# A hybrid RWKV-7 layer on one core: the recurrent chain's VectorE and ScalarE operations placed 400 places further forward by the scheduler

## The chip, the cores and the metric

The kernel runs on one core of a Trainium2 chip. The metric is the device time of one execution in microseconds, taken as the median of several runs. A profiled execution gives the trace, in which every instruction of the engines has its start and its duration. The engines are called PE (TensorE, the matrix engine), DVE (VectorE), ACT (ScalarE), POOL (GpSimd) and SP (SyncE, which issues most transfers). Each works through its own queue of instructions in the order in which the program writes them.

## What is computed

One layer of a decoder on 1024 tokens of width 1024. The normalised input goes through one large projection, whose columns feed three branches: an RWKV-7 time mixing (16 heads of 64), a convolution module and a cross-attention into 256 memory tokens. The branches are projected, gated, summed and projected once more. What matters here is the time mixing, which is a recurrence over tokens:

```python
def wkv7_scan(r, decay, k, v, a_vec, b_vec):
    def step(state, inp):
        r_t, w_t, k_t, v_t, a_t, b_t = inp
        sa = jnp.einsum('bhvk,bhk->bhv', state, a_t)
        state = (state * w_t[:, :, None, :]
                 + sa[..., :, None] * b_t[:, :, None, :]
                 + v_t[..., :, None] * k_t[:, :, None, :])
        y = jnp.einsum('bhvk,bhk->bhv', state, r_t)
        return state, y
    _, ys = lax.scan(step, s0, seqs)
...
    h = rms_norm(x, g_norm)
    proj = h @ w_all
...
    wkv = wkv7_scan(rh, decay, kh, vh, -kk, kk * ah)
    wkv = (wkv - mu) * lax.rsqrt(var + RWKV_GN_EPS)
    y_rwkv = ((wkv * gn_g + gn_b + bonus) * jax.nn.silu(rwkv_gate)) @ w_proj_rwkv
```

## The kernel before

**Dense work.** The projections are done tile by tile by `g_dense`: a tile of 128 output columns for 1024 tokens in two halves of 512, each half 24 matmuls of 128x128 by 128x512 (L291, result d). Each weight tile is split into a high part wh (ACT, L123) and a low part wl (DVE, L124, 128x1024), and three products of parts are summed. Of the next tile's weights, wl is made while the tile before is multiplied.

**The recurrence.** It is computed in chunks of 64 tokens. The heads go in pairs j = 0 to 7 and the 1024 tokens in halves e = 0 and 1, so there are 16 blocks, numbered 2j + e, with eight chunks each. Four generators write the work of a block:
- `g_prep` makes the decayed r, k and their products: L480 and L486 (decays), L515 to L534 (ar, u, bk, ks, rs) on DVE, L529 and L533 on POOL, L545 on PE.
- `g_sub` solves the triangular systems inside the chunks. POOL scales U by rb (L574, 128x1024). Then DVE does 31 steps of two small operations, tm = W x U (L580) and W += tm (L583). Transposes (L600) and two groups of small matmuls (L608, L618) follow, with copies on ACT.
- `g_pre` prepares the chain's operands for four chunks at a time (L633 to L673).
- `g_chain` carries the 64x64 state s through the chunks: ry = s x ar on PE (L702), sav = ry + Y on DVE (L703), sas = sav x tk on PE (L710), and the new s on DVE (L713, two halves), with sp = s x pc on ACT (L706). After four chunks come the output's matmuls (L724) and their copy (L726). At the block's end the head's mean and variance are made on DVE (L731 to L748), the inverse root on POOL (`rsqrt`, L114 and L118), and DVE normalises Y (L753, L754); PE transposes it (L759), and DVE makes o from it (L761, L762), which is stored.

**What sets the order.** Beside a block's chain run the solve of the next block, the preparation of the one after it and some tiles of dense work. The function `mix` asks the generators in turn for a piece, by their shares of the stage. This is the order in which the instructions are written. A scheduler then takes them from a heap, the lowest number first, among those whose operands come from instructions already placed; the number is the place in which an instruction was written, and inside `tc.high_priority(n)` it is n lower. What comes out is the fixed order of each engine's queue. Behind the recurrence, from some 1080 us of the trace on, come the convolution, the attention and the last projections.

Of the kernel before, what the change touches and what calls it, by code (L numbers as in the profile page):

```python
# [12 lines left out]
AF = mybir.ActivationFunctionType  # L13
ALU = mybir.AluOpType
# [4 lines left out]
P = 128  # L19
# [5 lines left out]
C = 64  # L25
# [33 lines left out]
N_VEC = _n  # L59


@with_exitstack
def hybrid_kernel(ctx: ExitStack, tc: tile.TileContext, x: bass.AP, mem: bass.AP, wt: bass.AP,
                  vecs: bass.AP, wup: bass.AP, gfin: bass.AP, out: bass.AP):
    nc = tc.nc
    act, dve, pool, pe = nc.scalar, nc.vector, nc.gpsimd, nc.tensor


    const = ctx.enter_context(tc.tile_pool(name="const", bufs=1))
# [259 lines left out]
    with tc.tile_pool(name="rk", bufs=1, reuse_waits="tile") as rk:  # L329
# [53 lines left out]
        def fl(ap):  # L383
            return ap.rearrange("p a t -> p (a t)")
# [243 lines left out]
        state = [0]  # L628

        def g_pre(j, e, q, g, bk, v, Y):  # L630
            tkp = bank("tr")
            for cc in range(4):
                pe.transpose(tkp[:, cc * P:(cc + 1) * P], fl(bk[:, q * 4 + cc, :, :]), ident)  # L633
            tk = rk.tile([P, 4, P], F32, name="tk", tag="tk", bufs=2)
            act.copy(tk, tkp.rearrange("p (c t) -> p c t", t=P))
            yield
            vtp = bank("tr")
            for cc in range(2):
                c = q * 4 + cc * 2
                pe.transpose(vtp[:, cc * P:(cc + 1) * P], v[:, c * C:(c + 2) * C], ident)  # L640
            sav = rk.tile([P, 4, P], F32, name="sav", tag="sav", bufs=2)
            for par in range(2):
                rows = slice(ko(par), ko(par) + C)
                act.copy(sav[rows, par::2, :], vtp[rows, 0:2 * P].rearrange("p (c t) -> p c t", t=P))
            yield
            zv = vtp[:, 2 * P:4 * P]
            u1 = bank("g", 2)
            uv = u1.rearrange("p (k c h t) -> p k c h t", k=2, c=2, h=2)
            for n in range(4):
                cc2, hh = n // 2, n % 2  # L650
                vsl = slice(hh * C, (hh + 1) * C)
# [16 lines left out]
            act.copy(fl(Y[:, q * 2:q * 2 + 2, :]), zv)  # L668
            for par in range(2):
                own = slice(so(par), so(par) + C)  # L670
                oth = slice(ko(par), ko(par) + C)
                act.copy(tk[own, par::2, :], uv[own, 0].rearrange("p c h t -> p c (h t)"))
                act.copy(g[own, par, :, q * 2:q * 2 + 2, oth], uv[own, 1].rearrange("p c h t -> p h c t"))  # L673
            yield (tk, sav)

        def g_chain(j, e):
            g, ar, bk, pc = GG.pop((j, e)), AR.pop((j, e)), BK.pop((j, e)), PCS.pop((j, e))
            v = VS.pop((j, e))
            if e == 0:
                dve.memset(s0[state[0]], 0.0)  # L680
# [10 lines left out]
            dve.tensor_tensor(out=bv, in0=bp, in1=v, op=ALU.mult)  # L691
            for q in range(2):
                tk, sav = got
                ry = bank("ry", 2)
                for cc in range(4):
                    c = q * 4 + cc
                    par = c % 2
                    cg = e * CPH + c
                    own = slice(so(par), so(par) + C)
                    cs = slice(cc * P, (cc + 1) * P)  # L700
                    S0, S1 = s0[state[0]], s0[1 - state[0]]
                    pe.matmul(ry[:, cs], lhsT=fl(ar[:, c, :, :]), rhs=S0, start=True, stop=True)  # L702
                    dve.tensor_tensor(out=sav[own, cc, :], in0=ry[own, cs], in1=Y[own, c // 2, :], op=ALU.add)  # L703
                    if cg < NCH - 1:
                        sp = rk.tile([P, P], F32, name="sp", tag="sp", bufs=1)
                        act.activation(sp, S0, AF.Copy, scale=pc[:, c:c + 1])  # L706
                    yield
                    if cg < NCH - 1:
                        sn = bank("sas")
                        pe.matmul(sn[:, 0:P], lhsT=tk[:, cc, :], rhs=sav[:, cc, :], start=True, stop=True)  # L710
                        for hh in range(2):
                            vsl = slice(hh * C, (hh + 1) * C)
                            dve.scalar_tensor_tensor(out=S1[vsl, vsl], in0=sn[vsl, vsl], scalar=pc[vsl, c:c + 1],  # L713
                                                     in1=sp[vsl, vsl], op0=ALU.mult, op1=ALU.add)
# [11 lines left out]
                act.copy(fl(Y[:, q * 2:q * 2 + 2, :]), yp[:, 0:2 * P])  # L726
                yield
                ryv = ry.rearrange("p (c t) -> p c t", t=P)
                for par in range(2):
                    oth = slice(ko(par), ko(par) + C)  # L730
                    dve.tensor_tensor(out=Y[oth, q * 2:q * 2 + 2, :], in0=Y[oth, q * 2:q * 2 + 2, :],  # L731
                                      in1=ryv[oth, par::2, :], op=ALU.add)
                for c2 in range(q * 2, q * 2 + 2):
                    for hh in range(2):
                        dve.bn_stats(out=st[:, c2, hh, :], in_=Y[:, c2, hh * C:(hh + 1) * C])
                yield

            n2 = CPH
# [4 lines left out]
            dve.tensor_tensor(out=mn, in0=stv[:, :, 1], in1=stv[:, :, 4], op=ALU.add)  # L743
            dve.tensor_tensor(out=df, in0=stv[:, :, 1], in1=stv[:, :, 4], op=ALU.subtract)
            dve.tensor_scalar(out=mn, in0=mn, scalar1=0.5, scalar2=None, op0=ALU.mult)
            dve.tensor_tensor(out=vr, in0=stv[:, :, 2], in1=stv[:, :, 5], op=ALU.add)
            dve.tensor_tensor(out=df, in0=df, in1=df, op=ALU.mult)
# [499 lines left out]
```

## Time and profile before

| | us |
|---|---|
| median of 3 runs | 1961.04 |
| lowest and highest run | 1960.19, 1962.81 |
| the profiled execution | 1960.84 |
| its span in the trace | 1959.0 |
| PE busy | 1848.2 (94% of the span) |
| DVE busy | 1411.1 (72%) |
| ACT busy | 693.2 (35%) |
| POOL busy | 226.5 (12%) |

The span runs from the first instruction to the last; 1.84 us of the execution lie outside it. An engine's busy time leaves out the time in which it waits. In the trace a PE matmul's duration reaches over the start of the next one, since they are pipelined; the distance from start to start is what it costs. In the rows of the timelines, a bracket at the end is the time that the engine was idle before the instruction, and what ended the wait.

### The profile page before, as it was taken

Reading aid. Unit: us, or ns where it says so; the run is one execution under the profiler, and the core shown is the slowest. Engines: PE = TensorE matmul, PEld = TensorE weight load, DVE = VectorE, ACT = ScalarE, POOL = GpSimd, SP = SyncE. Lnnn points to the kernel's source line nnn. Section 1 sums busy time; section 2 is a strip of 40 time slices with the busy share of each in tenths; the row PEclk is TensorE's granted clock in tenths of the full one; section 3 lists DMA queues with packets and bytes.
Section 4 is the critical chain, followed back from the end, with each engine's and each line's share of the span. In section 5 each row is a group of like instructions: output and inputs, shape, how many; then the busy total and the mean of one; then the engine's idle time right before and its main releaser. Section 6 shows DMA issues by size and latency. Waiting matters only on the chain. (4 is left out here: it accounts for less than half of the span.)

```text
span 1959.0 us, 30018 instructions
## 1 busy us (share of the span) xinstructions
PE 1848.2 (94%) x11412; PEld 1472.8 (75%) x11412; DVE 1411.1 (72%) x3028; ACT 693.2 (35%) x1303; POOL 226.5 (12%) x311
## 2 busy tenths in 40 slices
PE   6999998989899899989999999999999999999998
PEld 5777766767676676667788888888888787778887
DVE  6667787777778777787636998898999748644423
ACT  6334343443344344334334313232313435432121
POOL 2201111111111111111000000000000213100001
PEclk9999999999999999999999999999999999999999
DMA  4232212122121212212224411212123646775332
GB/s 147 58 97 63 71 36 68 54 61 68 48 86 36 66 56 58 71 42 79 71 78 140 132 46 42 75 54 76 54 76 108 233 163 221 256 252 164 129 129 86
DMA packets 127936, 188.61 MB, mean 96 GB/s; under 512 B 64432, under 2 KB 66608, under 8 KB 127792
## 3 DMA queue, kind: packets, MB, share of 16 engines
q1 hardware_dynamic: 122704, 178.11, 29.0%
q10 hardware_dynamic: 4768, 8.07, 1.1%
q8 instruction: 89, 1.46, 0.3%
q0 software_dynamic: 320, 0.52, 0.1%
q14 instruction: 55, 0.45, 0.1%
HBM read 139.92 MB, written 46.20 MB: 95 GB/s over the span
## 5 line engine op out<-in xcount | busy, mean ns | idle before, releaser
L291 PE MATMUL d<-hH,wh 128*128 128x512 f32 x1552 | 626.0, 403 | 6.8 <-DVE cg L928 4.4
L291 PE MATMUL d<-hH,wl 128*128 128x512 f32 x1552 | 621.8, 401 | 0.0
L291 PE MATMUL d<-hL,wh 128*128 128x512 f32 x1552 | 619.1, 399 | 0.0
L291 PEld LDWEIGHTS d<-hH,wh 128*128 128x128 f32 x1552 | 294.1, 189 | 63.6 <-DVE cg L928 5.7
L291 PEld LDWEIGHTS d<-hH,wl 128*128 128x128 f32 x1552 | 294.1, 190 | 59.4 <-issue 0.2
L291 PEld LDWEIGHTS d<-hL,wh 128*128 128x128 f32 x1552 | 294.1, 189 | 56.2 <-issue 0.2
L841 DVE SCALAR_TENSOR_TENSOR ac<-up,wdw,ac 128x1024 f32<-128x1024 f32 x240 | 308.2, 1284 | 11.8 <-ACT ac L838 6.0
L123 ACT CAST wh<-wf 128x1024 fp32r<-128x1024 f32 x137 | 143.6, 1049 | 324.1 <-PE d L291 304.3
L124 DVE TENSOR_TENSOR wl<-wf,wh 128x1024 fp32r<-128x1024 f32 x137 | 176.8, 1291 | 95.7 <-ACT wh L123 95.4
L291 PE MATMUL d<-oH,wh 128*128 128x512 f32 x384 | 152.5, 397 | 11.4 <-DVE mg L1101 7.4
L291 PE MATMUL d<-oH,wl 128*128 128x512 f32 x384 | 151.4, 394 | 0.0
L291 PE MATMUL d<-oL,wh 128*128 128x512 f32 x384 | 151.4, 394 | 0.0
L583 DVE TENSOR_TENSOR W<-W,tm 128x60 f32<-128x60 f32 (+24 forms) x496 | 112.4, 227 | 10.0
L580 DVE TENSOR_TENSOR tm<-W,U 128x60 f32<-128x60 f32 (+24 forms) x496 | 107.7, 217 | 11.1
L706 ACT ACTIVATE sp<-s,pc 128x128 f32<-128x128 f32 x120 | 48.3, 402 | 174.8 <-DVE s L713 137.6
L291 PEld LDWEIGHTS d<-oH,wh 128*128 128x128 f32 x384 | 72.9, 190 | 30.4 <-ACT y L1138 5.1
L710 PEld LDWEIGHTS sas<-sav,tk 128*128 128x128 f32 x240 | 38.4, 188 | 67.5 <-DVE sav L703 49.2
L710 PE MATMUL sas<-sav,tk 128*128 128x128 f32 x240 | 54.1, 307 | 34.1 <-DVE sav L703 32.4
L291 PEld LDWEIGHTS d<-oH,wl 128*128 128x128 f32 x384 | 72.8, 190 | 16.1
L291 PEld LDWEIGHTS d<-oL,wh 128*128 128x128 f32 x384 | 72.8, 189 | 15.4
L713 DVE SCALAR_TENSOR_TENSOR s<-sas,pc,sp 64x64 f32<-64x64 f32 x240 | 67.6, 282 | 21.5 <-PE sas L710 16.1
L703 DVE TENSOR_TENSOR sav<-ry,Y 64x128 f32<-64x128 f32 x128 | 36.8, 288 | 43.4 <-ACT Y L668 26.5
(277 smaller groups left out, 2608.7 us busy)
## 6 DMA issues: line engine op xcount, KB each, us to landing
wf<-in_wt_dram SPq DMA_DIRECT2D x137, 512.0 KB
g_d<-gt SPq DMA_DIRECT2D x48, 256.0 KB
U<-ud SPq DMA_DIRECT2D x64, 128.0 KB
nxt<-in_x_dram SPq DMA_DIRECT2D x8, 512.0 KB
o_rwkv_d<-o SPq DMA_DIRECT2D x16, 256.0 KB
cv_d<-ac SPq DMA_DIRECT2D x8, 512.0 KB
o_mem_d<-om SPq DMA_DIRECT2D x16, 256.0 KB
xs<-cv_d SPq DMA_DIRECT2D x8, 512.0 KB
```

The lines of the kernel that those rows point to most:

```text
L123: act.copy(hi, src)
L124: (eng or dve).tensor_tensor(out=lo, in0=src, in1=hi.bitcast(F32), op=ALU.subtract)
L291: pe.matmul(po, lhsT=l[:, ks_], rhs=r[:, k, sl], start=(n == 0), stop=(n == 3 * KT - 1))
L580: dve.tensor_tensor(out=tv, in0=W[:, 0:m, i:i + 1].broadcast_to([NG * 32, m, n]), in1=U[:, i:i + 1, i + 1:32].broadcast_to([NG * 32, m, n] ...
L583: dve.tensor_tensor(out=wv_, in0=wv_, in1=tv, op=ALU.add)
L703: dve.tensor_tensor(out=sav[own, cc, :], in0=ry[own, cs], in1=Y[own, c // 2, :], op=ALU.add)
L706: act.activation(sp, S0, AF.Copy, scale=pc[:, c:c + 1])
L710: pe.matmul(sn[:, 0:P], lhsT=tk[:, cc, :], rhs=sav[:, cc, :], start=True, stop=True)
L713: dve.scalar_tensor_tensor(out=S1[vsl, vsl], in0=sn[vsl, vsl], scalar=pc[vsl, c:c + 1], in1=sp[vsl, vsl], op0=ALU.mult, op1=ALU.add)
L841: dve.scalar_tensor_tensor(out=ac, in0=up[:, tap:tap + S], scalar=wdw[:, tap * 8 + j:tap * 8 + j + 1], in1=ac, op0=ALU.mult, op1=ALU.add)
```

## The change

The operations of `g_pre` and `g_chain` on DVE and ACT, and the `rsqrt` of `g_chain` on POOL, are each issued inside `tc.high_priority(400)`. The matmuls and the transfers aren't. Since a helper issues them, the wrapped operations have the helper's line L73 in the changed kernel, and the other lines are some 16 higher (L291 is L307, L580 is L596, L702 is L718, L710 is L726, L724 is L740, L759 is L776).

```diff
+AHEAD = 400
...
+class Urgent:
+    def __init__(self, tc, eng):
+        self._tc, self._eng = tc, eng
+
+    def __getattr__(self, op):
+        f = getattr(self._eng, op)
+
+        def call(*args, **kw):
+            with self._tc.high_priority(AHEAD):
+                return f(*args, **kw)
+        return call
...
+    act_u, dve_u, pool_u = Urgent(tc, act), Urgent(tc, dve), Urgent(tc, pool)
...
-            act.copy(tk, tkp.rearrange("p (c t) -> p c t", t=P))
+            act_u.copy(tk, tkp.rearrange("p (c t) -> p c t", t=P))
...
-                    dve.tensor_tensor(out=sav[own, cc, :], in0=ry[own, cs], in1=Y[own, c // 2, :], op=ALU.add)
+                    dve_u.tensor_tensor(out=sav[own, cc, :], in0=ry[own, cs], in1=Y[own, c // 2, :], op=ALU.add)
...
-                        act.activation(sp, S0, AF.Copy, scale=pc[:, c:c + 1])
+                        act_u.activation(sp, S0, AF.Copy, scale=pc[:, c:c + 1])
...
-            dve.scalar_tensor_tensor(out=vr, in0=df, scalar=16.0, in1=vr, op0=ALU.mult, op1=ALU.add)
-            rsqrt(vr, vr, 1.0 / C, GN_EPS)
+            dve_u.scalar_tensor_tensor(out=vr, in0=df, scalar=16.0, in1=vr, op0=ALU.mult, op1=ALU.add)
+            with tc.high_priority(AHEAD):
+                rsqrt(vr, vr, 1.0 / C, GN_EPS)
```

All other operations of the two generators on DVE and ACT are changed in the same way. No instruction is added or removed. Of PE's 9356 instructions 1344 stand at another place of its queue, of DVE's 3030 it is 1207, of ACT's 1273 it is 167, of SP's 781 it is 93 and of POOL's 316 it is 6, all of them inside the recurrence.

The first place is DVE's queue behind the end of block 6, an even one: o is the block's output, tm and W are steps of the solve for a later block, sav and s_0 belong to the chain of the next block. Before:

```order
L762 SCALAR_TENSOR_TENSOR o<-o,vec,sg 128x512
L703 TENSOR_TENSOR sav<-ry,Y 64x128
L580 TENSOR_TENSOR tm<-W,U 128x31
L583 TENSOR_TENSOR W<-W,tm 128x31
L713 SCALAR_TENSOR_TENSOR s_0_405<-sas,pc,sp 64x64
L580 TENSOR_TENSOR tm<-W,U 128x30
```

And now:

```order
L73 SCALAR_TENSOR_TENSOR o<-o,vec,sg 128x512
L596 TENSOR_TENSOR tm<-W,U 128x31
L599 TENSOR_TENSOR W<-W,tm 128x31
L596 TENSOR_TENSOR tm<-W,U 128x30
L599 TENSOR_TENSOR W<-W,tm 128x30
L596 TENSOR_TENSOR tm<-W,U 128x29
L599 TENSOR_TENSOR W<-W,tm 128x29
L596 TENSOR_TENSOR tm<-W,U 128x28
L599 TENSOR_TENSOR W<-W,tm 128x28
L596 TENSOR_TENSOR tm<-W,U 128x54
L73 TENSOR_TENSOR sav<-ry,Y 64x128
```

Nine steps of the solve, which were spread behind the first sav, stand ahead of it.

The second place is PE's queue at the end of block 8: L724 is the output's matmuls, L759 the transposes of the block's end, L702 the first matmul of the next block's chain, and d the dense work. The first rows are those around L724, the last those around L759. Before:

```order
L618 MATMUL tr<-zt,wb 32x32 x16
L291 MATMUL d<-hH,wh 128x512
L291 MATMUL d<-hL,wh 128x512
L291 MATMUL d<-hH,wl 128x512
L291 MATMUL d<-hH,wh 128x512
L724 MATMUL tr<-sav,g 64x64 x8
...
L291 MATMUL d<-hL,wh 128x512
L759 MATMUL tr<-ident,Y 128x128 x4
L702 MATMUL ry<-s_0_405,ar 128x128
```

Between L724 and L759 stand 25 rows of L291. And now, with the middle of it where L718 stands:

```order
L740 MATMUL tr<-sav,g 64x64 x8
...
L307 MATMUL d<-hL,wh 128x512
L718 MATMUL ry<-s_0_405,ar 128x128
L307 MATMUL d<-hH,wl 128x512
L307 MATMUL d<-hH,wh 128x512
L307 MATMUL d<-hL,wh 128x512
L307 MATMUL d<-hH,wl 128x512
L307 MATMUL d<-hH,wh 128x512
L307 MATMUL d<-hL,wh 128x512
L307 MATMUL d<-hH,wl 128x512
L776 MATMUL tr<-ident,Y 128x128 x4
```

Between L740 and L776 stand 17 rows of L307 and one of L718, and the rows around L624 and L634 (L608 and L618 before) have 15 more of dense work between them that stood behind L724.

The third place is POOL's queue at the end of block 5, an odd one: vr is the variance, U the next solve's matrix. The same is changed in block 9, and nowhere else on this engine. Before:

```order
L567 MEMSET W_4908 128x256
L573 COPY W_4908<-rb_4909 32x8 x4
L574 TENSOR_TENSOR U_4907<-U_4907,rb_4909 128x1024
L114 TENSOR_SCALAR vr_4859<-vr_4859 128x8
L118 TENSOR_TENSOR vr_4859<-vr_4859,nhalf_97 128x8
```

And now:

```order
L583 MEMSET W_4908 128x256
L589 COPY W_4908<-rb_4909 32x8 x4
L130 TENSOR_SCALAR vr_4859<-vr_4859 128x8
L134 TENSOR_TENSOR vr_4859<-vr_4859,nhalf_97 128x8
L590 TENSOR_TENSOR U_4907<-U_4907,rb_4909 128x1024
```

The scaling of U has moved from ahead of the inverse root to directly behind it.

## Rows read from the trace of the kernel before

**Rows 1.** Window sums, the recurrence: busy us of each engine.

```profile
core 0: us, PE busy (x) PEld busy (x) DVE busy (x) ACT busy (x) POOL busy (x), PEclk, DMA share, GB/s
60.00:1140.00 1080.00, 1007.59 (x7611) 781.54 (x7610) 809.73 (x2320) 415.22 (x848) 142.54 (x215) 0.99 0.24 69
```

**Rows 2.** PE's waits from 60 to 1140 us: total, times, longest.

```profile
PE sas L710 <- DVE sav L703: 32.4, 43, 1.8
PE tr L759 <- DVE Y L754: 19.1, 6, 3.3
```

**Rows 3.** Timeline of DVE, even tail: start, duration, engine, line, operation.

```profile
641.64 1.22 DVE L124 TENSOR_TENSOR wl<-wf,wh 128x1024 fp32r<-128x1024 f32 x1
...
645.36 2.82 DVE L754 TENSOR_TENSOR Y<-Y,vr 128x512 f32<-128x512 f32 x1 [1.10 <-POOL vr L118]
```

**Rows 4.** Timeline of POOL, U at an odd and an even tail.

```profile
581.27 2.38 POOL L574 TENSOR_TENSOR U<-U,rb 128x1024 f32<-128x1024 f32 x1 [4.78 <-DMA U<-ud]
...
643.68 1.65 POOL L118 TENSOR_TENSOR vr<-vr,nhalf 128x8 f32<-128x8 f32 x1
645.29 2.34 POOL L574 TENSOR_TENSOR U<-U,rb 128x1024 f32<-128x1024 f32 x1
```

**Rows 5.** Timeline of PE, even tail of block 8.

```profile
638.57 0.69 PE L724 MATMUL tr<-sav,g 128*64 128x64 f32 x16
639.18 0.50 PE L291 MATMUL d<-hL,wh 128*128 128x512 f32 x1
...
644.76 0.39 PE L291 MATMUL d<-hL,wh 128*128 128x512 f32 x1
648.32 0.94 PE L759 MATMUL tr<-ident,Y 128*128 128x128 f32 x4 [3.17 <-DVE Y L754]
```

**Rows 6.** Timeline of PE, odd tail of block 7.

```profile
585.78 0.69 PE L724 MATMUL tr<-sav,g 128*64 128x64 f32 x16
...
592.55 0.63 PE L759 MATMUL tr<-ident,Y 128*128 128x128 f32 x4 [1.03 <-DVE W L583]
```

**Rows 7.** Timeline of DVE, the same odd tail.

```profile
591.71 0.69 DVE L754 TENSOR_TENSOR Y<-Y,vr 128x512 f32<-128x512 f32 x1 [1.94 <-POOL vr L118]
```

**Rows 8.** Timeline of DVE, start of a stretch S1.

```profile
535.88 0.75 DVE L762 SCALAR_TENSOR_TENSOR o<-o,vec,sg 128x512 f32<-128x512 f32 x1
539.82 0.29 DVE L703 TENSOR_TENSOR sav<-ry,Y 64x128 f32<-64x128 f32 x1 [3.19 <-ACT Y L668]
540.14 0.19 DVE L580 TENSOR_TENSOR tm<-W,U 128x31 f32<-128x31 f32 x1
540.37 0.19 DVE L583 TENSOR_TENSOR W<-W,tm 128x31 f32<-128x31 f32 x1
```

**Rows 9.** Timeline of PE, the chain's matmuls in the same S1.

```profile
544.51 0.49 PE L710 MATMUL sas<-sav,tk 128*128 128x128 f32 x2 [0.32 <-DVE sav L703]
...
546.91 0.38 PE L702 MATMUL ry<-s,ar 128*128 128x128 f32 x2
...
554.89 0.49 PE L710 MATMUL sas<-sav,tk 128*128 128x128 f32 x2 [1.47 <-DVE sav L703]
...
562.22 0.46 PE L710 MATMUL sas<-sav,tk 128*128 128x128 f32 x2 [0.47 <-DVE sav L703]
...
567.81 0.49 PE L710 MATMUL sas<-sav,tk 128*128 128x128 f32 x2 [0.83 <-DVE sav L703]
```

**Rows 10.** Timeline of PE, the chain's matmuls in a stretch S0.

```profile
617.09 0.49 PE L710 MATMUL sas<-sav,tk 128*128 128x128 f32 x2 [0.88 <-DVE sav L703]
...
619.85 0.49 PE L702 MATMUL ry<-s,ar 128*128 128x128 f32 x2 [0.42 <-DVE s L713]
...
623.26 0.49 PE L702 MATMUL ry<-s,ar 128*128 128x128 f32 x2 [0.46 <-DVE s L713]
```

**Rows 11.** Timeline of DVE, long operations in the same S0.

```profile
621.35 0.68 DVE L527 TENSOR_TENSOR ks<-ks,ta 128x512 f32<-128x512 f32 x1
...
623.48 0.74 DVE L534 SCALAR_TENSOR_TENSOR rs<-rs,vec,ks 128x512 f32<-128x512 f32 x1
...
625.67 1.22 DVE L124 TENSOR_TENSOR wl<-wf,wh 128x1024 fp32r<-128x1024 f32 x1
```

More of the change, by code (lines that the diff above doesn't have):

```diff
@@ L643, in g_pre @@
                 rows = slice(ko(par), ko(par) + C)
-                act.copy(sav[rows, par::2, :], vtp[rows, 0:2 * P].rearrange("p (c t) -> p c t", t=P))
+                act_u.copy(sav[rows, par::2, :], vtp[rows, 0:2 * P].rearrange("p (c t) -> p c t", t=P))
             yield
@@ L667, in g_pre @@
                               rhs=g[own, par, hh, q * 2 + cc2, oth], start=True, stop=True)
-            act.copy(fl(Y[:, q * 2:q * 2 + 2, :]), zv)
+            act_u.copy(fl(Y[:, q * 2:q * 2 + 2, :]), zv)
             for par in range(2):
@@ L671, in g_pre @@
                 oth = slice(ko(par), ko(par) + C)
-                act.copy(tk[own, par::2, :], uv[own, 0].rearrange("p c h t -> p c (h t)"))
-                act.copy(g[own, par, :, q * 2:q * 2 + 2, oth], uv[own, 1].rearrange("p c h t -> p h c t"))
+                act_u.copy(tk[own, par::2, :], uv[own, 0].rearrange("p c h t -> p c (h t)"))
+                act_u.copy(g[own, par, :, q * 2:q * 2 + 2, oth], uv[own, 1].rearrange("p c h t -> p h c t"))
             yield (tk, sav)
@@ L679, in g_chain @@
             if e == 0:
-                dve.memset(s0[state[0]], 0.0)
+                dve_u.memset(s0[state[0]], 0.0)
             Y = rk.tile([P, 4, P], F32, name="Y", tag="Y", bufs=1)
@@ L690, in g_chain @@
             bv = rk.tile([P, HS], F32, name="bv", tag="bv", bufs=1)
-            dve.tensor_tensor(out=bv, in0=bp, in1=v, op=ALU.mult)
+            dve_u.tensor_tensor(out=bv, in0=bp, in1=v, op=ALU.mult)
             for q in range(2):
@@ L712, in g_chain @@
                             vsl = slice(hh * C, (hh + 1) * C)
-                            dve.scalar_tensor_tensor(out=S1[vsl, vsl], in0=sn[vsl, vsl], scalar=pc[vsl, c:c + 1],
+                            dve_u.scalar_tensor_tensor(out=S1[vsl, vsl], in0=sn[vsl, vsl], scalar=pc[vsl, c:c + 1],
                                                      in1=sp[vsl, vsl], op0=ALU.mult, op1=ALU.add)
@@ L725, in g_chain @@
                                   rhs=sav[:, cc2 * 2 + par, hh * C:(hh + 1) * C], start=True, stop=True)
-                act.copy(fl(Y[:, q * 2:q * 2 + 2, :]), yp[:, 0:2 * P])
+                act_u.copy(fl(Y[:, q * 2:q * 2 + 2, :]), yp[:, 0:2 * P])
                 yield
@@ L730, in g_chain @@
                     oth = slice(ko(par), ko(par) + C)
-                    dve.tensor_tensor(out=Y[oth, q * 2:q * 2 + 2, :], in0=Y[oth, q * 2:q * 2 + 2, :],
+                    dve_u.tensor_tensor(out=Y[oth, q * 2:q * 2 + 2, :], in0=Y[oth, q * 2:q * 2 + 2, :],
                                       in1=ryv[oth, par::2, :], op=ALU.add)
@@ L734, in g_chain @@
                     for hh in range(2):
-                        dve.bn_stats(out=st[:, c2, hh, :], in_=Y[:, c2, hh * C:(hh + 1) * C])
+                        dve_u.bn_stats(out=st[:, c2, hh, :], in_=Y[:, c2, hh * C:(hh + 1) * C])
                 yield
@@ L742, in g_chain @@
             df = rk.tile([P, n2], F32, name="df", tag="df", bufs=1)
[L743 to L747, printed above, removed]
-            dve.scalar_tensor_tensor(out=vr, in0=df, scalar=16.0, in1=vr, op0=ALU.mult, op1=ALU.add)
-            rsqrt(vr, vr, 1.0 / C, GN_EPS)
+            dve_u.tensor_tensor(out=mn, in0=stv[:, :, 1], in1=stv[:, :, 4], op=ALU.add)
+            dve_u.tensor_tensor(out=df, in0=stv[:, :, 1], in1=stv[:, :, 4], op=ALU.subtract)
+            dve_u.tensor_scalar(out=mn, in0=mn, scalar1=0.5, scalar2=None, op0=ALU.mult)
+            dve_u.tensor_tensor(out=vr, in0=stv[:, :, 2], in1=stv[:, :, 5], op=ALU.add)
+            dve_u.tensor_tensor(out=df, in0=df, in1=df, op=ALU.mult)
+            dve_u.scalar_tensor_tensor(out=vr, in0=df, scalar=16.0, in1=vr, op0=ALU.mult, op1=ALU.add)
+            with tc.high_priority(AHEAD):
+                rsqrt(vr, vr, 1.0 / C, GN_EPS)
             for _ in range(GNW):
@@ L752, in g_chain @@
             yv = Y.rearrange("p c (h v) -> p (c h) v", h=2)
-            dve.tensor_tensor(out=yv, in0=yv, in1=mn[:, :, None].broadcast_to([P, n2, C]), op=ALU.subtract)
-            dve.tensor_tensor(out=yv, in0=yv, in1=vr[:, :, None].broadcast_to([P, n2, C]), op=ALU.mult)
+            dve_u.tensor_tensor(out=yv, in0=yv, in1=mn[:, :, None].broadcast_to([P, n2, C]), op=ALU.subtract)
+            dve_u.tensor_tensor(out=yv, in0=yv, in1=vr[:, :, None].broadcast_to([P, n2, C]), op=ALU.mult)
             for _ in range(GNW):
@@ L760, in g_chain @@
             o = rk.tile([P, HS], F32, name="o", tag="o", bufs=2)
-            dve.scalar_tensor_tensor(out=o, in0=ytp, scalar=vcol("gn_g", j), in1=bv, op0=ALU.mult, op1=ALU.add)
-            dve.scalar_tensor_tensor(out=o, in0=o, scalar=vcol("gn_b", j), in1=SG.pop((j, e)),
+            dve_u.scalar_tensor_tensor(out=o, in0=ytp, scalar=vcol("gn_g", j), in1=bv, op0=ALU.mult, op1=ALU.add)
+            dve_u.scalar_tensor_tensor(out=o, in0=o, scalar=vcol("gn_b", j), in1=SG.pop((j, e)),
                                      op0=ALU.add, op1=ALU.mult)
```

## The prediction

> **What bounds the kernel now.** I read the window sums first, to find where TensorE (PE) is not busy. From 60 to 1140 us, the stretch of the recurrence, PE works 1007.59 of 1080 us, so 72.4 us are idle there [rows 1]. The order of every engine behind that stretch is the same in both kernels, so the change can only give or take parts of these 72.4 us. PE has a full queue of projection matmuls (L291, one each 0.23 us: 25 of them start between 639.18 and 644.76 [rows 5]), executed strictly in the order written; it idles only where a matmul of the recurrence stands in its queue before its operand is ready. The table of waits says where [rows 2]: 32.4 us at L710, which waits for sav (L703) on VectorE (DVE), and 19.1 us in six waits of up to 3.3 us at L759, the transposes at a block's end, which wait for L754. The recurrence runs through 16 blocks (head pair j, half e), two in each 115 us. I call the end of a block with e=0 an even tail and of one with e=1 an odd tail, the stretch behind an even tail S1 and behind an odd tail S0. The timelines then give one of each.
>
> **How the change works.** No instruction is added or removed, so the busy times stay. The wrapped operations are placed further forward in the engines' queues, and the operations of the other generators (the triangular solve's tm and W at L580 and L583, the preparation's L515 to L534, the weights' wl at L124) fall back; PE's order follows. Each place is priced by its own waits.
>
> **Even tails (six, blocks 2 to 12).** Now L724 starts at 638.57 and ends 0.69 later at 639.26, L759 starts at 648.32: 9.06 us, of which PE covers 5.89 with 25 dense matmuls and waits 3.17 [rows 5]. In that path DVE has wl, 1.22 us, ahead of L748 [rows 3]. In the changed order wl and sg are ahead of the whole tail and L748 comes directly behind L753; that is the odd tail's order of today, where the same path from L724's end (585.78 + 0.69) to L759 at 592.55 takes 6.08 us [rows 6]. One thing keeps the even tail longer. On GpSimd (POOL), U (L574) starts at 645.29 as the power L118 ends, and L754, which starts at 645.36, takes 2.82 us [rows 3, 4] instead of the 0.69 of the odd tail [rows 7]: 2.13 us more. So the path becomes 6.08 + 2.13 = 8.21. The cover shrinks too, because the order puts L724 later and L759 earlier in the dense matmuls: 17 of them and one L702 stand between, 5.89 - 8 x 0.23 + 0.22 = 4.27 (0.22 is my estimate for the short L702, a dense matmul's pitch). The wait becomes 8.21 - 4.27 = 3.94 in place of 3.17, **+0.8 each, +4.8 for six**. The shorter path is thus spent, because the dense work was drawn ahead of L724 where nothing waited. Bounds: -0.8 (the cover stays at 5.89, wait 2.32) and +1.9 (wl's wait for its weights moves in front of the whole tail, its 1.22 us without cover).
>
> **Odd tails 5 and 9 (two).** Here POOL's order changes: U, which now starts long before (10 us ahead of L754 in block 7, at 581.27 against 591.71) [rows 4, 7], stands directly behind L118. Then L754 meets it as at an even tail, 2.82 for 0.69, and three dense matmuls fewer lie between L724 and L759: 2.13 + 3 x 0.23 = **+2.8 each, +5.7**. In odd tails 3, 7 and 11 POOL keeps its order and one more dense matmul lies ahead of L759: -0.23 each, **-0.7**.
> The row shows only that L754 is long when U started 0.07 us earlier. The Trainium skill ("SBUF — State Buffer", Who interferes with whom) has a rule for that: a VectorE instruction with two inputs in SBUF and a GpSimd instruction that reads SBUF exclude each other on a shared port, and whoever issues first keeps it for the whole instruction. It speaks against this change, since it makes two more blocks depend on which of them issues first. By it an L754 behind U would end at U's end plus its own 0.69, at 648.32; the trace has 648.18, so it agrees within 0.14, and the term would be 2.3 for 2.13.
>
> **S1 (seven, behind block 0 and the even tails).** After the last o (L762, 535.88 + 0.75) DVE idles 3.19 us until the first sav at 539.82, because that sav stands ahead of the solve's tm and W, which could run [rows 8]. In the changed order nine of these stand ahead of sav; with 0.23 from one to the next [rows 8] that is 2.1 us of work moved into idle time. PE's waits for sav behind it are 0.32, 1.47, 0.47 and 0.83, in all 3.09 [rows 9]. They don't all go. The order now also has the third sav ahead of the two L515, and that sav can't run before its L702, which starts at 546.91 behind PE's dense matmuls [rows 9]: DVE stands still there with L515 behind it, and loses most of what it was ahead. From there to the sav in front of the wait of 1.47, I count in the changed order 6.9 us of DVE work with the durations of the trace. It would end at about 554.2 where it now ends at 554.84 (PE resumes at 554.89 [rows 9]): 0.6 less. I estimate the four as 0.2, 0.85, 0.1 and 0.6 and a new one of 0.15, in all 1.9: **-1.2 each, -8.4**. Bounds: nothing, and all 3.09, which is -21.6 for seven.
>
> **S0 (six, behind odd tails).** Here DVE has little idle time to fill. PE waits 0.88, 0.42 and 0.46 [rows 10]. The order draws three long operations forward with the chain: L527 (0.68) ahead of the sav that is now in front of it, L534 (0.74) ahead of an s (L713), and wl (1.22) ahead of the last s [rows 11]; two to four short tm and W go behind in exchange. The first two waits then go from 1.30 to 0.75, since short operations leave the front of sav. The three long ones add 0.68 - 0.4, 0.74 - 0.4 and 1.22 less a cover of 1.0 by PE's four dense matmuls: 0.3 + 0.3 + 0.25. In all +0.3, **+1.8 for six**. Bounds: -1.0 each (the first gain twice over, no loss), +0.7 (no short operation leaves).
>
> **Sum.** 4.8 + 5.7 - 0.7 - 8.4 + 1.8 = +3.2 us. The profiled execution took 1960.84, 1.84 of it outside its span of 1959.0, and the median is 1961.04; both lead to **1964 us**.
>
> **The rivals.**
> Slower, by the long operations (L527, L534, wl) in front of the state chain. For it: DVE is strictly in order and has 809.73 us of work in these 1080 [rows 1]; each wait at L710 is one where sav is late. If the tm and W moved behind are nearly free because they overlap their neighbours, L527 costs its whole 0.68, and S0 comes to +0.65 each (+3.9), while S1 gives only the 0.4 of its worst wait (-2.8). Sum 4.8 + 5.7 - 0.7 - 2.8 + 3.9 = +10.9: 1972 us. It decides as soon as the time from a sav to the next s on DVE exceeds PE's cover there, some 1.4 us (six dense matmuls). Against it: in S1 the idle 3.19 us are real.
> Faster: the waits at L710 are what the change aims at, and the seven S1 lose 2.2 of 3.09 each (-15.4), because the third sav doesn't hold up DVE (its L702 comes earlier as all of PE comes earlier); S0 gives 0.5 each (-3.0). With the tails at +9.8 that is -8.6: 1952 us. Against it: L702 has a fixed place among the dense matmuls.
> The lock doesn't happen in blocks 5 and 9: if L754 issues 0.1 us earlier than U, it lasts 0.69 as in [rows 7], and the sum is 3.2 - 4.3 = -1.1: 1960 us, no change. For it: the margin in the row is 0.07 us. Against it: it went the same way in all six even tails [rows 2].
>
> **How the numbers follow.** Forecast 0.42, its own range 1959 to 1968; slower rival 0.25 (1972); faster rival 0.20 (1952); no lock 0.13 (1960). The range 1953 to 1972 leaves out half of the slower rival and half or a little more of the faster one, some 0.2. No change means within 0.2%, 3.9 us, about what a measurement here can tell. Faster: the faster rival and a little of the forecast's low end, 0.24. Slower (over 1965): the slower rival and a third of the forecast, 0.40. Within: 0.36.
>
> **What would show it.** In the profile after: six waits at L759's line of 3.9 us where they were 3.2, and two new ones of the same size in blocks 5 and 9, with L754 at 2.8 us eight times and not six; DVE's 3.19 us of idle ahead of an S1's first sav down to about 1, and the wait of 1.47 in S1 near 0.85; in S0 new waits behind L527 and wl. PE's idle time from 60 to 1140 would be about 75.6 in place of 72.4. I am wrong if the waits at L710 fall from 32.4 to under 20 (then faster), or if they rise (then the long operations count in full).

## The result, and the profile after

The changed kernel takes 1974.51 us in the median of four runs (1973.79 to 1975.66), the kernel before 1961.57 beside it: a ratio of 1.0065, with a 95% interval of 1.005 to 1.008. It is slower by 12.9 us, outside the predicted range. The profiled execution of the changed kernel took 1974.09 us, with a span of 1972.4.

The window sums, cut where the last block's transposes start (L759, now L776: the end of the recurrence), first for the kernel before, then for the changed one. The columns are stretch, its length, and busy us with instructions of PE, weight load, DVE, ACT and POOL, then PE's granted clock and DMA.

```profile
0.00:1034.40 1034.40, 947.58 (x7260) 727.48 (x7261) 754.23 (x2297) 408.29 (x845) 152.56 (x244) 0.99 0.24 67
1034.40:1959.00 924.60, 900.65 (x4152) 745.29 (x4152) 656.92 (x731) 284.93 (x458) 73.92 (x67) 0.99 0.39 129
```

```profile
0.00:1050.37 1050.37, 957.23 (x7260) 731.42 (x7261) 766.44 (x2297) 407.40 (x845) 155.24 (x244) 0.98 0.23 66
1050.37:1972.40 922.03, 899.08 (x4152) 745.08 (x4152) 655.36 (x731) 285.10 (x458) 74.72 (x67) 0.99 0.39 129
```

The recurrence ends 15.97 us later. Of that, 6.3 us are waits of PE (1050.37 - 957.23 = 93.1 against 1034.40 - 947.58 = 86.8), and 9.65 us are busy time, with the same 7260 matmuls. The second part, in the same order in both kernels, is 2.6 us shorter. It differs as much between other profiles of this study (921.2 to 926.9), so nothing is made of it.

The waits of PE from 60 to 1152 us, the rows that answer to [rows 2], and behind them two rows of the kernel before that [rows 2] leave out:

```profile
PE tr L776 <- DVE Y L73: 31.5, 8, 3.9
PE sas L726 <- DVE sav L73: 27.2, 42, 1.9
PE ry L718 <- DVE s L73: 7.7, 18, 0.7
PE tr L776 <- DVE W L599: 3.4, 4, 1.0
```

```profile
PE tr L759 <- DVE W L583: 6.2, 6, 1.0
PE ry L702 <- DVE s L713: 5.8, 13, 0.9
```

The ends of the blocks have eight long waits in place of six, 12.4 us more, and four short ones in place of six, 2.8 us less. The state chain waits 5.2 us less for sav (L726) and 1.9 more for s (L718), in all 3.3 less.

The timeline of PE at the end of block 8, against [rows 5]:

```profile
649.40 0.69 PE L740 MATMUL tr<-sav,g 128*64 128x64 f32 x16
650.02 0.50 PE L307 MATMUL d<-hL,wh 128*128 128x512 f32 x1
...
654.03 0.40 PE L307 MATMUL d<-hH,wl 128*128 128x512 f32 x1
658.37 1.09 PE L776 MATMUL tr<-ident,Y 128*128 128x128 f32 x4 [3.94 <-DVE Y L73]
659.11 0.78 PE L307 MATMUL d<-hH,wh 128*128 128x512 f32 x1
659.68 0.63 PE L307 MATMUL d<-hL,wh 128*128 128x512 f32 x1
660.11 0.63 PE L307 MATMUL d<-hH,wl 128*128 128x512 f32 x1
...
662.25 0.39 PE L307 MATMUL d<-hH,wh 128*128 128x512 f32 x1
662.48 0.39 PE L307 MATMUL d<-hL,wh 128*128 128x512 f32 x1
```

The path from L740's end (650.09) to L776 is 8.28 us, and the wait is 3.94. Behind the wait a dense matmul starts every 0.43 us, until 662 us, and then every 0.23 again. The window sums over the same place show the granted clock (third number from the end):

```profile
652.00:654.00 2.00, 2.00 (x11) 1.70 (x10) 1.25 (x8) 0.22 (x1) 0.47 (x2) 1.00 0.00 0
...
658.00:660.00 2.00, 1.63 (x6) 1.56 (x7) 0.73 (x2) 0.00 (x0) 0.00 (x0) 0.59 0.00 0
660.00:662.00 2.00, 2.00 (x9) 1.51 (x8) 1.83 (x7) 0.00 (x0) 0.00 (x0) 0.56 0.05 17
662.00:664.00 2.00, 2.00 (x32) 1.56 (x30) 0.61 (x4) 1.22 (x3) 0.00 (x0) 1.00 0.65 245
```

For some 3.4 us PE runs at the lower of its two levels, 1.2 GHz in place of 2.4. In windows of 1 us from 60 to 1160 us I count 13 such stretches in the changed kernel, six in the kernel before. Eleven of the 13 begin at the eight waits of 3.94, within the wait or up to 1.2 us behind it (at three of the waits there are two in a row). In the kernel before, five of the six waits of 3.2 us have one. Of the rest, one stands at 92 us in both kernels, and one at 201 us in the changed kernel alone, behind a wait of the chain of 1.94 us.

The odd end of block 5, timelines of POOL, DVE and PE:

```profile
478.15 1.64 POOL L134 TENSOR_TENSOR vr<-vr,nhalf 128x8 f32<-128x8 f32 x1
479.76 2.34 POOL L590 TENSOR_TENSOR U<-U,rb 128x1024 f32<-128x1024 f32 x1
```

```profile
479.83 2.82 DVE L73 TENSOR_TENSOR Y<-Y,vr 128x512 f32<-128x512 f32 x1 [2.12 <-POOL vr L134]
```

```profile
482.79 1.09 PE L776 MATMUL tr<-ident,Y 128*128 128x128 f32 x4 [3.94 <-DVE Y L73]
```

U starts as the inverse root ends, L754 (L73 here) 0.07 us later, and L754 takes 2.82 us where it took 0.69. The wait was 1.03 in odd ends [rows 6].

S1. The first sav behind the end of block 8, timeline of DVE, before and now:

```profile
655.30 0.29 DVE L703 TENSOR_TENSOR sav<-ry,Y 64x128 f32<-64x128 f32 x1 [4.47 <-ACT Y L668]
```

```profile
665.34 0.29 DVE L73 TENSOR_TENSOR sav<-ry,Y 64x128 f32<-64x128 f32 x1 [2.62 <-ACT Y L73]
```

Nine steps of the solve now run in DVE's idle time, which is 1.85 us shorter. (The 3.19 of [rows 8] stand behind block 6, the one end in the kernel before with no fall of the clock.) The chain on PE in S1 behind block 6, against [rows 9]:

```profile
562.24 0.49 PE L726 MATMUL sas<-sav,tk 128*128 128x128 f32 x2 [0.96 <-DVE sav L73]
...
569.81 0.46 PE L726 MATMUL sas<-sav,tk 128*128 128x128 f32 x2 [0.52 <-DVE sav L73]
...
575.30 0.49 PE L726 MATMUL sas<-sav,tk 128*128 128x128 f32 x2 [0.74 <-DVE sav L73]
...
582.06 0.49 PE L718 MATMUL ry<-s,ar 128*128 128x128 f32 x2 [0.64 <-DVE s L73]
```

The wait of 1.47 became 0.96, and a new one of 0.64 appears at L718; all waits of PE in this S1 sum to 3.1, for 3.2 before. The window sums from the first sas matmul of this S1 to the one with the longest wait show why, before and now:

```profile
540.26:554.89 14.63, 12.85 (x104) 10.09 (x104) 13.91 (x47) 10.16 (x23) 2.09 (x4) 1.00 0.21 66
```

```profile
549.90:562.24 12.34, 11.25 (x96) 8.30 (x96) 11.91 (x35) 9.86 (x23) 1.95 (x3) 1.00 0.09 28
```

DVE (third number with an x) has 2.0 us less to do on this way, about the 2.1 that the nine steps promised; but PE (the first) has 1.6 us less as well, eight matmuls fewer. The difference, 0.4, is nearly what the wait lost. S0, PE's chain, against [rows 10]:

```profile
624.83 0.49 PE L726 MATMUL sas<-sav,tk 128*128 128x128 f32 x2 [0.47 <-DVE sav L73]
...
627.40 0.49 PE L718 MATMUL ry<-s,ar 128*128 128x128 f32 x2 [0.25 <-DVE s L73]
...
629.58 0.49 PE L726 MATMUL sas<-sav,tk 128*128 128x128 f32 x2 [0.53 <-DVE sav L73]
```

The waits of 0.88 and 0.42 became 0.47 and 0.25, in sum 0.72 where 0.75 was forecast. The one of 0.46 is gone, and one of 0.53 is new at the sas just ahead of its place, whose sav now stands behind ks (L543, L527 before) on DVE:

```profile
628.52 0.69 DVE L543 TENSOR_TENSOR ks<-ks,ta 128x512 f32<-128x512 f32 x1
629.25 0.28 DVE L73 TENSOR_TENSOR sav<-ry,Y 64x128 f32<-64x128 f32 x1
```

### The profile page after: what moved, and what is told of

It is laid out like the page before. It is cut to its first block, busy times and chain, and to the rows that moved or that the text cites. A ratio compares the mean times of both kernels' runs of the same rounds, so it can differ in the third digit from the quotient of the medians.

```text
span 1972.4 us, 30022 instructions
## 1 busy us (share of the span) xinstructions
PE 1856.3 (94%) x11412; PEld 1476.5 (75%) x11412; DVE 1421.8 (72%) x3028; ACT 692.5 (35%) x1303; POOL 230.0 (12%) x311
## 4 chain that ended last, share of the span: by engine, by line
PE 60%; DVE 24%; DMA 5%; issue 4%; ACT 3%; POOL 2%; SPq 0%; DVEq 0%; POOLq 0%; ACTq 0%
PE d L307 44%; PE d L228 4%; DVE tm L596 3%; DVE W L599 3%; DVE Y L73 3%; DVE s L73 2%; PE g L228 2%; DVE wl L140 2%; DMA ost<-o_rwkv_d 2%; PE g L561 1%; PE ry L904 1%; DVE sav L73 1%; POOL vr L134 1%; PE ry L228 1%; DVE g L564 1%
## 5 line engine op out<-in xcount | busy, mean ns | idle before, releaser
L307 PE MATMUL d<-hH,wh 128*128 128x512 f32 x1552 | 629.1, 405 | 7.3 <-DVE cg L945 4.9
L307 PE MATMUL d<-hH,wl 128*128 128x512 f32 x1552 | 625.1, 403 | 0.0
L307 PE MATMUL d<-hL,wh 128*128 128x512 f32 x1552 | 621.2, 400 | 0.0
L307 PEld LDWEIGHTS d<-hH,wh 128*128 128x128 f32 x1552 | 295.5, 190 | 64.1 <-DVE cg L945 6.2
L307 PEld LDWEIGHTS d<-hH,wl 128*128 128x128 f32 x1552 | 295.3, 190 | 58.4 <-issue 0.2
L307 PEld LDWEIGHTS d<-hL,wh 128*128 128x128 f32 x1552 | 295.6, 190 | 56.2 <-issue 0.2
L307 PE MATMUL d<-oH,wh 128*128 128x512 f32 x384 | 152.5, 397 | 9.5 <-DVE mg L1118 7.1
L307 PE MATMUL d<-oH,wl 128*128 128x512 f32 x384 | 151.9, 395 | 0.0
L307 PE MATMUL d<-oL,wh 128*128 128x512 f32 x384 | 151.7, 395 | 0.0
L596 DVE TENSOR_TENSOR tm<-W,U 128x60 f32<-128x60 f32 (+24 forms) x496 | 107.8, 217 | 12.6
L599 DVE TENSOR_TENSOR W<-W,tm 128x60 f32<-128x60 f32 (+24 forms) x496 | 107.4, 216 | 12.9
L73 ACT ACTIVATE sp<-s,pc 128x128 f32<-128x128 f32 x120 | 48.3, 403 | 152.2 <-DVE s L73 151.9
L307 PEld LDWEIGHTS d<-oH,wh 128*128 128x128 f32 x384 | 73.0, 190 | 27.9 <-issue 5.7
L307 PEld LDWEIGHTS d<-oH,wl 128*128 128x128 f32 x384 | 72.9, 190 | 16.0
L307 PEld LDWEIGHTS d<-oL,wh 128*128 128x128 f32 x384 | 72.9, 190 | 15.5
L726 PEld LDWEIGHTS sas<-sav,tk 128*128 128x128 f32 x240 | 39.1, 188 | 58.5 <-DVE sav L73 40.9
L73 DVE SCALAR_TENSOR_TENSOR s<-sas,pc,sp 64x64 f32<-64x64 f32 x240 | 67.4, 281 | 18.2 <-PE sas L726 14.6
L726 PE MATMUL sas<-sav,tk 128*128 128x128 f32 x240 | 53.2, 303 | 28.1 <-DVE sav L73 27.2
L718 PEld LDWEIGHTS ry<-s,ar 128*128 128x128 f32 x256 | 43.8, 189 | 33.9 <-DVE s L73 27.8
```

The source lines that it names most:

```text
L73: return f(*args, **kw)
L307: pe.matmul(po, lhsT=l[:, ks_], rhs=r[:, k, sl], start=(n == 0), stop=(n == 3 * KT - 1))
L596: dve.tensor_tensor(out=tv, in0=W[:, 0:m, i:i + 1].broadcast_to([NG * 32, m, n]), in1=U[:, i:i + 1, i + 1:32].broadcast_to([NG * 32, m, n] ...
L599: dve.tensor_tensor(out=wv_, in0=wv_, in1=tv, op=ALU.add)
```

## Experiments

Theory A is that the loss is the longer and added waits at the blocks' ends, and the stretches at half clock that they bring. Theory B is that PE's added busy time comes from the new neighbours in its queue.

**U with one input, in both orders.** U is multiplied by 0 in place of rb, so the solve's result is left out. All engines keep their order in both kernels.

```diff
-            pool.tensor_tensor(out=U, in0=U, in1=rb[:, None, :].broadcast_to([NG * 32, 32, 32]), op=ALU.mult)
+            pool.tensor_scalar(out=U, in0=U, scalar1=0.0, scalar2=None, op0=ALU.mult)
```

On the changed kernel:

> The changed kernel with every engine's order kept, but U (L590 of the changed kernel) is multiplied by the constant 0 in place of rb, so that the GpSimd instruction has one input instead of two (the solve's result is left out). Theory A (waits and clock): the two long parts of the loss are the waits of 3.94 us at L776, of which L754's 2.8 us is the larger part, and the stretches at half of TensorE's clock behind them (13 in the profile after, 6 before, about 1.4 us each). If the shorter U takes 1 to 2 us off each of the eight waits, that is 8 to 17 us, and most stretches at half clock go too, up to 15 us more: 1943 to 1955. Theory B (TensorE's 9.6 us more of busy time in the recurrence come from the new neighbours in its queue, not from the clock): only the waits go, 1957 to 1966, and the busy time stays above that of the kernel before.

On the kernel before:

> The kernel before with every engine's order kept and the same edit of U. Theory A: six waits of 3.2 us lose 1 to 2 us each (6 to 13) and the five stretches at half clock behind them go (7): 1942 to 1950, and the changed order with the same edit is within 3 us of it. Theory B: 1949 to 1955, and the changed order with the same edit stays some 8 us behind it.

Measured: the changed order 1956.23 us (0.9983 of the kernel before, interval 0.9966 to 0.9999), between the ranges of the two theories, and the order before 1942.26 (0.9912, 0.9889 to 0.9935), in the range of theory A. U did not get shorter, as I had expected (2.78 us for 2.34), but L754 takes 1.52 us for 2.82. The end of block 8 in the changed order (timeline of PE, window sums), then the same in the order before:

```profile
649.47 0.63 PE L776 MATMUL tr<-ident,Y 128*128 128x128 f32 x4 [2.65 <-DVE Y L73]
...
650.00:654.00 4.00, 4.00 (x15) 3.07 (x15) 2.93 (x10) 0.59 (x1) 0.52 (x1) 0.59 0.35 131
```

```profile
641.16 0.63 PE L759 MATMUL tr<-ident,Y 128*128 128x128 f32 x4 [1.87 <-DVE Y L754]
...
641.00:645.00 4.00, 3.84 (x38) 3.17 (x40) 1.52 (x3) 1.49 (x4) 1.21 (x1) 1.00 0.23 74
```

In the profiled executions, waits of 2.65 us still bring the lower clock, in all eight places; waits of 1.85 to 1.88 don't, in five places, and one of 1.98 did. The sums up to the last transposes, changed order and order before:

```profile
0.00:1035.46 1035.46, 953.89 (x7261) 727.78 (x7261) 747.51 (x2297) 407.92 (x845) 162.97 (x244) 0.99 0.23 67
```

```profile
0.00:1020.40 1020.40, 942.59 (x7260) 723.20 (x7261) 739.05 (x2297) 408.12 (x845) 159.64 (x244) 1.00 0.24 68
```

In the order before, the same matmuls in the same order took 947.58 and now 942.59: 5.0 us for four stretches fewer (six to two, one of the two at 30 us, ahead of the windows counted above), beside 9.0 us less of waits. That part of the expectation by theory A came true, and theory B can't explain it. The expected tie between the two orders did not come, and by the times alone the pair is nearer to theory B's 8 us: the orders differ by 14. The traces say where it is: 11.3 us are busy time, with seven stretches more at half clock (nine to two), which at the 1.6 us each worked out below would be 11.2. The changed order loses because its waits are 0.8 us longer, enough to bring the clock down.

The executions of the changed order bear this out. The two with a mean granted clock of 0.996 and 0.997 took 1949.12 and 1949.96 us, the eight others, at 0.990 to 0.993, 1954.75 to 1961.60: the same instructions in the same order, some 8 us apart with the clock. So a wait of 2.65 us doesn't seem to bring the clock down every time.

**Matmuls in the waits.**

```diff
             ytp = bank("tr")
+            for _ in range(16 if 0 < 2 * j + e < 13 else 0):
+                pe.matmul(ytp, lhsT=bones, rhs=hH[:, 0, 0:HS], start=True, stop=True)
```

> The changed kernel with 16 more matmuls (the size of L291, 0.23 us each, result overwritten) ahead of the transposes at the end of blocks 1 to 12, to fill TensorE's waits there without making them shorter. Theory A: the time that the waits take stays, but the clock doesn't fall behind them: 11 of the 13 stretches at half clock go, about 15 us, 1958 to 1963; at the odd ends without a long wait the added work costs up to 2 us each, so up to 1969. Theory B: no gain, 1974 or more.

Measured: 1968.44 us (1.005, interval 1.0035 to 1.0065), inside theory A's wider bound of 1969. The stretches behind the ends are gone, two of 13 are left. But the run doesn't tell the theories apart: the added work changed the order, U now starts behind L754 at the even ends, and L754 takes 0.69 in all blocks. POOL at the end of block 8:

```profile
657.38 2.40 POOL L590 TENSOR_TENSOR U<-U,rb 128x1024 f32<-128x1024 f32 x1 [11.06 <-DMA U<-ud]
```

**U behind L754 at the even ends of the kernel before.**

```diff
+            if e == 0 and j > 0:
+                pool.tensor_copy(U[:, 31, 31:32], DONE.pop())
             pool.tensor_tensor(out=U, in0=U, in1=rb[:, None, :].broadcast_to([NG * 32, 32, 32]), op=ALU.mult)
...
+            if e == 0 and j < KT - 1:
+                yd = rk.tile([P, 1], F32, name="yd", tag="yd", bufs=2)
+                pool.tensor_copy(yd, Y[:, 0, 0:1])
+                DONE.append(yd)
             for _ in range(GNW):
                 yield
             ytp = bank("tr")
```

> The kernel before with U's multiplication at the end of the even blocks made to wait for L754, by two copies of one column on GpSimd. Theory A: L754 takes 0.69 there, so six waits lose 2.1 us (13) and the clock stays up behind them (7): 1941 to 1948. Rival: the solve starts 0.8 us later and the wait turns up in its steps or in the next chain: 1953 to 1961.

Measured: 1941.81 us (0.9907, interval 0.9887 to 0.9927), as theory A had it. Timelines of DVE, POOL and PE at the end of block 8 (the added lines shift the numbers: L758 is L754, L767 is L759, L578 is U's line):

```profile
639.17 0.69 DVE L758 TENSOR_TENSOR Y<-Y,vr 128x512 f32<-128x512 f32 x1 [1.10 <-POOL vr L118]
```

```profile
639.93 0.19 POOL L761 COPY yd<-Y 128x1 f32<-128x1 f32 x1 [0.79 <-DVE Y L758]
640.18 0.19 POOL L577 COPY U<-yd 128x1 f32<-128x1 f32 x1
640.45 2.39 POOL L578 TENSOR_TENSOR U<-U,rb 128x1024 f32<-128x1024 f32 x1
```

```profile
640.01 0.63 PE L767 MATMUL tr<-ident,Y 128*128 128x128 f32 x4 [1.05 <-DVE Y L758]
```

The wait of 3.17 is 1.05, by just the 2.13 that L754 is shorter, and no stretch at half clock is left at any end. U starts 1.3 us behind L754's start and nobody waits for it. This version beats both kernels.

**Priority without the blocks' ends.** The operations from L724's output on lose the priority (`dve_u` and `act_u` become `dve` and `act` from the copy of yp on, and `rsqrt` stands alone again).

```diff
-                act_u.copy(fl(Y[:, q * 2:q * 2 + 2, :]), yp[:, 0:2 * P])
+                act.copy(fl(Y[:, q * 2:q * 2 + 2, :]), yp[:, 0:2 * P])
...
-            with tc.high_priority(AHEAD):
-                rsqrt(vr, vr, 1.0 / C, GN_EPS)
+            rsqrt(vr, vr, 1.0 / C, GN_EPS)
```

> The changed kernel with the blocks' ends left as before: from L724's output on, nothing is issued with priority, only g_pre and the state chain are. By the order, GpSimd's U is back ahead of vr at the end of blocks 5 and 9, and the even ends keep the 17 dense matmuls between L724 and L759 that the changed kernel has. Theory A: two waits of 3.9 become 0.8 (6 us), and three or four stretches at half clock go (4 to 6): 1963 to 1966. Rival (the chain's own order is what costs): 1971 or more. Second rival (the operations of the blocks' ends were the whole loss): 1961.

Measured: 1967.45 us (1.0043, interval 1.0026 to 1.006), a little above the range of theory A and below that of the rival. The waits at the odd ends of blocks 5 and 9 are 0.81 and those at the six even ends still 3.94, with seven stretches at half clock behind these. So the state chain's priority alone gives the even ends their 17 dense matmuls, and the priority of the ends is needed for what happens in blocks 5 and 9. By the order, the priority of `g_pre` alone moves nothing on PE, DVE and POOL, and that of `rsqrt` moves nothing at all.

**The same with U behind L754 at the even ends** (the edits of the fourth and the fifth run together).

> The kernel of the run without priority at the blocks' ends, with U made to wait for L754 at the even ends as in the fourth run. Theory A: no L754 of 2.8 us is left, the waits at the even ends are 0.8 longer than the 1.05 of the fourth run (fewer dense matmuls between), 1.8 in all, too short for a fall of the clock or just at it; the waits inside the blocks are 0.6 shorter per block. 1940 to 1944, within 2 us of the fourth run; 1950 if the clock falls at 1.8. Rival (the chain's order costs by itself): 1948 or more with the clock up.

Measured: 1945.15 us (0.9924, interval 0.991 to 0.9939), 1 us above the range of theory A. The waits at the even ends (L783 is L759 here), and the clock behind one of them:

```profile
PE tr L783 <- DVE Y L774: 10.9, 6, 1.8
...
645.00:649.00 4.00, 3.45 (x23) 2.77 (x25) 3.15 (x4) 0.62 (x2) 2.77 (x3) 1.00 0.00 0
```

Six waits of 1.82, and the clock stays at 1.00 behind all six. The chain's order is then some 3 us behind the fourth run, with overlapping intervals: it brings neither the gain that it is for nor a loss of size. The chain waits 1.7 us less than in the fourth run (38.7 for 40.4 us), the even ends 4.6 us more (10.9 for 6.3).

**Priority for the blocks' ends alone** (`g_pre` and the state chain without, the rest of `g_chain` with).

```diff
-                    dve_u.tensor_tensor(out=sav[own, cc, :], in0=ry[own, cs], in1=Y[own, c // 2, :], op=ALU.add)
+                    dve.tensor_tensor(out=sav[own, cc, :], in0=ry[own, cs], in1=Y[own, c // 2, :], op=ALU.add)
...
-                        act_u.activation(sp, S0, AF.Copy, scale=pc[:, c:c + 1])
+                        act.activation(sp, S0, AF.Copy, scale=pc[:, c:c + 1])
```

> The changed kernel with priority only for the blocks' ends (from L724's output on). By the order, U is ahead of vr in blocks 5 and 9, and the dense matmuls between L724 and L759 are as many as before. Theory A: nothing that costs is in it: 1959 to 1963, six stretches at half clock as before. Rival (the operations of the ends bring U behind vr on the chip or make the waits longer): 1966 or more.

Measured: 1957.24 us (0.9989, interval 0.998 to 0.9999), some 2 us below the range, with six waits of 3.2 and six stretches at half clock, as before.

**The whole change with U behind L754 at the even ends** (the edit of the fourth run on the changed kernel).

> The changed kernel as it is, with U made to wait for L754 at the even ends. By the order, U is ahead of vr again in blocks 5 and 9, and between L724 and L759 stand 17 or 18 dense matmuls in blocks 2, 4 and 6, but only 12 in blocks 8, 10 and 12. Theory A: L754 is 0.69 throughout; the waits at L759 are about 1.8 in blocks 2, 4 and 6 and 1.2 more, about 3.0, in blocks 8, 10 and 12, with a stretch at half clock behind each of these three and none behind the others: 1948 to 1955. Rival (the clock doesn't go by TensorE's wait): no stretch there, or one behind every end, 1945 or 1960.

Measured: 1967.54 us (1.0027, interval 1.0016 to 1.0038): above the range. The waits are as expected, 1.82 to 1.86 in blocks 2 to 6 and 3.22 in blocks 8 to 12. The window sums behind blocks 4 and 8:

```profile
424.00:428.00 4.00, 4.00 (x43) 3.23 (x42) 3.35 (x6) 1.31 (x3) 2.58 (x2) 1.00 0.02 4
...
657.00:661.00 4.00, 4.00 (x15) 2.74 (x14) 2.25 (x5) 0.59 (x1) 2.38 (x2) 0.57 0.00 0
```

The clock falls behind all three long waits (twice in a row behind one), not behind those of blocks 2 and 4, but also behind one of 1.86 in block 6. Beyond that, PE's busy time up to the last transposes is 960.11 here and 944.48 in the sixth run, with the same matmuls. Five stretches more explain some 8 of these 15.6 us. The scheduler made another order here, with 20 dense matmuls drawn from between the ends of blocks 13 and 14 into earlier places; what the other 7 us are stays open. L754 takes 0.69 us in all blocks of this run, so even without a long L754 the whole change gains nothing.

**Priority for the blocks' ends alone, and U behind L754 at the even ends** (the edits of the fourth and the seventh run).

> Priority only for the blocks' ends, with U made to wait for L754 at the even ends. Theory A: 25 and 20 dense matmuls at the ends as in the kernel before, waits of 1.0, no fall of the clock: 1938 to 1943, the fourth run or a little better. Rival (the operations of the ends draw other work in front of the chain once the lock is gone): 1945 or more.

Measured: 1942.67 us (0.9903, interval 0.9887 to 0.9919), not to be told from the fourth run.

## Why the prediction was wrong

**The step that failed** is the first sentence of "How the change works": "No instruction is added or removed, so the busy times stay." PE's busy time rose by 9.65 us in the recurrence. The span rose by 13.4 us where the sum had 3.2: by these 9.65, by 6.3 of waits for the 3.2, and by 2.6 less in the second part. The sum counted PE's waits and nothing that comes behind a wait. What comes behind is the lower clock, and the rows of the kernel before held it: L759 took 0.94 us behind a wait of 3.17 [rows 5] and 0.63 behind one of 1.03 [rows 6]. (At the four other falls L759 took 0.63 to 0.81, since the clock fell behind its start; there the dense matmuls that follow show it, most of them 0.63 us in place of 0.39.) The price could have been read from the same trace, because one of the six even ends, that of block 6, has the same wait and no fall. The window sums from its L759 to the next, and from block 8's:

```profile
534.42:592.55 58.13, 53.93 (x434) 41.18 (x435) 41.82 (x140) 22.43 (x48) 8.44 (x13) 1.00 0.28 78
648.32:708.03 59.71, 55.51 (x434) 42.56 (x435) 41.67 (x140) 22.54 (x48) 8.46 (x13) 0.97 0.27 76
```

The same 434 matmuls in the same order take 53.93 and 55.51 us: 1.6 us for one stretch. Seven more stretches would be 11 us by that; 9.65 were measured. The doubled ones cost less, as the same order with one stretch in the first run shows. From the end of block 5 to the next, two stretches and then one:

```profile
482.79:542.64 59.85, 53.99 (x422) 40.98 (x423) 47.06 (x142) 23.46 (x50) 8.80 (x13) 0.96 0.18 47
477.36:534.90 57.54, 52.95 (x422) 40.06 (x423) 45.78 (x142) 23.49 (x50) 9.29 (x14) 0.97 0.18 49
```

The second stretch costs 1.0 us there, and 1.3 and 0.7 behind blocks 10 and 12. Four single stretches at 1.6 and these three are 9.4 us, an estimate. Little is left for theory B: the sixth run, with the changed order inside the blocks, has 944.48 us of busy time up to the last transposes and the fourth 941.64, and the sixth has one stretch more, so the new neighbours cost some 1 us, an estimate from one profile of each. The Trainium skill ("TensorE: Matmul & The Clock Gate", Part 1) says that the clock drops to 1.2 GHz when the engine has been idle. The traces agree (a granted clock of 0.5 at five of the six waits of 3.2 us in the kernel before), and the prediction should have weighed this rule beside the one on the shared port.

**The waits, term by term** (predicted, then measured between the starts of L759 and L776):
- Even ends +4.8, measured +4.5. The wait of 3.94 was met to the hundredth, the path of 8.21 is 8.28.
- Odd ends of blocks 5 and 9 +5.7, measured +5.8; the lock came as in the row, U first by 0.07 us, so the rival without a lock is out.
- Odd ends of 3, 7 and 11 -0.7, measured -0.7 (1.03 to 0.81).
- S1 -8.4, measured -1.2, of which -1.4 stand behind block 0 and +0.1 behind the six even ends together: the term is near nothing there. Behind block 6, DVE won the 2.0 us of lead that the nine steps promised, and the third sav, which I had holding it up, did not stand idle. What failed is the silent assumption that PE's dense matmuls stay where they are between the chain's: the order moved eight of PE's matmuls out of the same stretch, so 1.6 of the 2.0 us only made the stretch shorter for both engines. Sums of the solve's steps that are moved are not sums of waits that go.
- S0 +1.8, measured -2.8. Of the waits behind the long operations that were drawn forward, the one behind L527 came (0.53 us in the S0 shown, for 0.85 forecast of all three), those behind L534 and wl did not, and the wait of 0.46 went. Each S0 has 1.7 to 2.0 us of waits in place of 2.3 to 2.4.

S1 and S0 together are -4.0 for -6.6: S1 missed by 7.2 us and S0 by 4.6 the other way. With 0.7 us ahead of block 0's end the waits rose by 6.3. That this is only 3 us more than the sum is in part luck.

**The rivals.** The slower rival gave 1972 us by long operations in front of the chain. Its number is near, its mechanism is not what happened: the waits of the chain fell by 3.3 us. The faster rival is out as well. No rival had the clock, and so the range was too low at its upper end.

**Where the expected gain went.** The chain's priority does shorten its waits, by 3.3 us. It pays for this at the blocks' ends, where PE's dense matmuls are used up earlier, and there each added wait costs its own length and a stretch at half clock.

## What to carry to other kernels

When a change lengthens a wait of TensorE, price what comes behind it too: look at the distance from one dense matmul to the next behind a short and a long wait, and at the granted clock in windows of 1 us, before setting up the sum. A reordering keeps the instruction counts but not the busy time. A preference for one chain in a scheduler moves the fillers of all others: here two copies of one column, which hold a GpSimd instruction back until a VectorE instruction is done, were worth 18 us (0.9907), and 400 places of priority for the chain that looked critical cost 13.

## What the runs showed of the hardware

- The clock fell behind 35 waits of 2.65 us and more out of 37 at the blocks' ends in the kernels whose waits are listed above (before, changed, first, fifth, seventh and eighth run; the two without are the 3.17 of block 6 in the kernel before and in the seventh run). Behind waits of 1.82 to 1.98 it stayed up in 13 of 15 (second, sixth and eighth run).
- A second stretch at half clock followed directly behind the first at three of the eight long waits of the changed kernel, though PE had work from the wait's end on. At these three the clock had fallen 0.9 to 2.0 us before the wait ended (windows of 0.2 us); at the other five it fell at most 0.4 us before the end, or behind it.
- U as an instruction with one input (first and second run), which starts 0.06 us ahead of L754, made L754 1.52 us in place of 0.69. U itself took 2.78 us, as it does where no L754 stands beside it (2.77 to 2.87 at the odd ends), so only L754 was slowed, and it ended 1.2 us ahead of U. With two inputs L754 took 2.82 and ended 0.55 us behind U, nearly as if it had started at U's end.
